# RWKV-7 chunk inverses in a diffusion backbone: the masked product copied into the inverse by four predicated copies, and other pauses around the products of inverses

## Chip, cores and metric

The kernel runs on one core of one Trainium2 chip. The metric is the device time of one execution in microseconds (us), shown as the median of three runs.

## What is computed

A backbone block with two layers over 256 context and 1024 latent tokens of width 1024, all in float32. Each layer has an input projection, three groups of heads (a gated linear attention, a windowed attention, and RWKV-7 time mixing in both directions), an output projection and a SwiGLU. The change lies in the RWKV group, whose recurrence the reference writes token by token:

```
def rwkv7_scan(r, w, k, v, kk, a, state0):
    def step(S, inp):
        rt, wt, kt, vt, kkt, at = inp
        sa = jnp.einsum('bhvk,bhk->bhv', S, kkt)
        S = (S * wt[:, :, None, :] - sa[..., None] * (kkt * at)[:, :, None, :]
             + vt[..., None] * kt[:, :, None, :])
        return S, jnp.einsum('bhvk,bhk->bhv', S, rt)
    S_final, o = lax.scan(step, state0, xs)
```

There are 4 heads of 64, two directions, and the state is a 64x64 matrix of each head.

## The kernel before

**The chunks.** The kernel works on chunks of 64 tokens, 20 in each layer. Within a chunk the recurrence becomes a triangular system of 64x64, one for each of the 4 heads and 2 directions; its inverse is needed. `u` counts four pairs (2 directions by 2 pairs of heads), and the two heads of a pair, or the halves of a block, lie on different partitions. Everything below is in the function `rwkv_mixer`.

**`prep` (L1183 on)** is a generator that makes the inverses. Iteration `i` begins the "young" chunk `i` and ends the "old" chunk `i - 1`, so that the two share instructions. In the order of the code:

1. `gram` multiplies the young chunk's four vectors on TensorE (`ps_g`) and VectorE multiplies the result by a triangular mask into `LQ` (128 partitions x 4 x 128). `X`, the inverse to be, starts as an identity of 32x32 blocks, written by GpSimd (`eye32`).
2. The first level of the inverse is the masked part of `LQ` itself. ScalarE copies its four 32x32 diagonal blocks, one for each group of 32 partitions, into a tile `ld`; one predicated copy on VectorE writes `ld` into `X` where the mask `lev1` is set; a VectorE transpose of 32x32 blocks makes `XT` (L1199 to L1203).
3. The old chunk's second Gram product goes to `MP` in the same way. GpSimd scales `Ke`.
4. `yield 3400`: see below.
5. Two steps, each of them: `py = LQ * XT` (`ps_y`, 32x32 products, 16 or 32 instructions), a ScalarE copy to `y`, `yield 1000`, `pz = y * X` (`ps_w`), a predicated copy of `pz` into `X` with the mask `lev2`, a transpose to `XT`, `yield 1200`. Step 0 and step 1 serve the young and the old chunk at once, which are at different levels.
6. For the old chunk a last product joins the 32x32 blocks to 64x64: 8 instructions of `ps_y` (called ps_y6 in the code), 4 transposes `ps_kt`, 8 of `ps_w`; the result is `XF`.

**`scan` (L1272 on)** follows with the state: `ps_r` from `MP` and from the state `SBD`, copies to `Rbd`, `ps_r` again with `XF`, copies to `VU` and `Ubd`, `ps_s`, and the state's update. Chunk `i` of the scan needs the inverse `i` and the scan of `i - 1`. `finish` normalizes a tile of finished tokens, with many small VectorE operations (`bn_stats`, a square root by integer arithmetic `rw_rs`, `fy`).

**`in_rest`** is the dense work beside it: the other 13 columns of the input projection, with 24 products of 128x128 by 512 (or 256) for each column and group of tokens (`ps_in`), each column with its own weight split (`w_hl`), drains, rotary positions (`rope`, L657 to L664) and the gates of the linear attention (`gl_`). The last column is held back until the scan has ended (`HOLD = 1`).

**What sets the order.** Class `Weave` runs these generators against each other and so writes TensorE's program by hand. `Tensor` keeps a count of modelled TensorE time `TE.t`; a generator that yields a number of ns is not resumed before that much modelled time has gone by, and whoever is ready by rank goes first: scan 0, prep 1, finish 3, dense work 9. So a pause in `prep` is filled with dense products, as long as there are any. The instructions of ScalarE, VectorE, GpSimd and the queues are put in order by the framework's own scheduler; those that `prep` and `scan` issue (`FIRST`) have a raised priority. All engines then run in their order and wait on semaphores.

Of the kernel before, what the change touches and what calls it, by code (L numbers as in the profile page):

```python
# [10 lines left out]
F32 = mybir.dt.float32  # L11
# [27 lines left out]
P = 128  # L39
# [106 lines left out]
def block_kernel(ctx: ExitStack, tc: tile.TileContext, a):  # L146
    nc = tc.nc
    V, S, G, SY = nc.vector, nc.scalar, nc.gpsimd, nc.sync
# [973 lines left out]
    def rwkv_mixer(l, t_first, pool, fpool, pp, spawn):  # L1122
# [7 lines left out]
        lev1 = pool.tile([P, 128], U8, name="lev1")  # L1130
# [19 lines left out]
        f2 = lambda ap: ap.rearrange("p u n -> p (u n)")  # L1150
# [5 lines left out]
        def gram(AK, w_, dst):  # L1156
            V = FIRST[0]
            ps = new([P, 4, P], "ps_g")
            for u in range(4):
                for hs in H:  # L1160
                    TE.matmul(ps[hs, u, :], AK[hs, u, w_, :], AK[hs, u, 0:2, :].rearrange("p s n -> p (s n)"))
            V.tensor_tensor(dst.rearrange("p (d q) n -> p d q n", d=2), ps.rearrange("p (d q) n -> p d q n", d=2),
                            mgr.unsqueeze(2).to_broadcast([P, 2, 2, P]), ALU.mult)
# [3 lines left out]
        def load(i):  # L1167
            b, cc = batch[i], (i, SIGC[i])

            AK = pool.tile([P, 4, 4, 64], F32, name="AK", bufs=4)  # L1170
            for d in range(2):
                SY.dma_start(AK[:, 2 * d:2 * d + 2], d_ab[:, 2 * d:2 * d + 2, cc[d]])
            Dt = pool.tile([P, 4], F32, name="Dt", bufs=4)
            for d in range(2):
                G.tensor_copy(Dt[:, 2 * d:2 * d + 2].unsqueeze(2), Dall[l][:, 2 * d:2 * d + 2, cc[d]:cc[d] + 1])
            b.update(cc=cc, AK=AK, Dt=Dt)
# [6 lines left out]
        def prep():  # L1183

            V, S, G = FIRST
            load(0)
            for i in range(NC + 1):
                yield after(("s", i - 3))
                p = i % 2
                young, old = batch[i] if i < NC else None, batch[i - 1] if i else None  # L1190
                hv = slice(0, 2) if i < NC and i else slice(p, p + 1) if old is None else slice(1 - p, 2 - p)
                if young is not None:
                    if i + 1 < NC:
                        load(i + 1)
                    X, XT = X2[:, p], XT2[:, p]
                    G.tensor_copy(X, eye32.unsqueeze(1).to_broadcast([P, 4, 32]))
                    young["LQ"] = LQ = pool.tile([P, 4, P], F32, name="LQ", bufs=3)
                    gram(young["AK"], 3, LQ)
                    ld = pool.tile([P, 4, 32], F32, name="ld")  # L1199
                    for r in range(0, 128, 32):  # L1200
                        S.copy(ld[r:r + 32], LQ[r:r + 32, :, r % 64:r % 64 + 32])
                    V.copy_predicated(f2(X), lev1, f2(ld))
                    V.transpose(f2(XT), f2(X))  # L1203
                if old is not None:
                    cc, Dt, AK = (old[n] for n in ("cc", "Dt", "AK"))
                    old["VU"] = VU = pool.tile([P, 512], F32, name="VU", bufs=3)
                    old["vb"] = vb = Vbd[p]
                    for d in range(2):
                        c = cc[d]
                        src = d_v[c % 2 * 64:c % 2 * 64 + 64, c // 2, :]  # L1210
                        SY.dma_start(VU[0:64, d * 256:(d + 1) * 256], src)
                        s4 = src.rearrange("s (q h n) -> s q h n", q=2, h=2)
                        for hp in range(2):
                            SY.dma_start(vb[H[hp], 2 * d:2 * d + 2, H[hp]], s4[:, :, hp, :])

                    Ke = pool.tile([P, 4, P], F32, name="Ke")
                    G.tensor_tensor(Ke, AK[:, :, 2:4, :].rearrange("p u w n -> p u (w n)"),
                                    Dt.unsqueeze(2).to_broadcast([P, 4, P]), ALU.mult)
                    old["MP"] = MP = pool.tile([P, 4, P], F32, name="MP", bufs=2)
                    gram(AK, 2, MP)  # L1220
                yield 3400 if young is not None else 0
                both = [(h, b["LQ"]) for h, b in ((p, young), (1 - p, old)) if b is not None]
                for step in range(2):
                    py = new([P, 2, 4, 32], "ps_y")
                    for h, LQ in both:
                        for u, rs, cs in blocks:
                            TE.matmul(py[rs, h, u, :], LQ[rs, u, cs], XT2[rs, h, u, :])
                    y = pool.tile([P, 2, 4, 32], F32, name="y", bufs=2)
                    S.copy(y[:, hv], py[:, hv])
                    yield 1000  # L1230
                    pz = new([P, 2, 4, 32], "ps_w")
                    for h, LQ in both:
                        for u, rs, cs in blocks:
                            TE.matmul(pz[rs, h, u, :], y[rs, h, u, :], X2[rs, h, u, :])
                    V.copy_predicated(f3(X2[:, hv]), lev2[:, step, p, hv].rearrange("p h n -> p (h n)"), f3(pz[:, hv]))
                    V.transpose(f3(XT2[:, hv]), f3(X2[:, hv]))
                    yield 1200
                if old is None:
                    continue

                X, XT, LQ, xf = X2[:, 1 - p], XT2[:, 1 - p], old["LQ"], XF[p]
                for r in (0, 32, 64, 96):
                    (S.copy if r < 64 else G.tensor_copy)(xf[r:r + 32, :, r % 64:r % 64 + 32], X[r:r + 32])
                ab = [(h, v, d) for v in range(2) for d in range(2) for h in (0, 64)]
                py = new([P, 2, 32], "ps_y6")
                for h, v, d in ab:
                    ra, rb = (h, h + 32) if d == 0 else (h + 32, h)
                    TE.matmul(py[rb:rb + 32, v, :], LQ[ra:ra + 32, 2 * d + v, rb % 64:rb % 64 + 32],
                              XT[ra:ra + 32, 2 * d + v, :])
                y = pool.tile([P, 2, 32], F32, name="y6")  # L1250
                S.copy(y, py)
                pt = new([P, 4, P], "ps_kt")
                for u in range(4):
                    TE.transpose(pt[:, u, :], Ke[:, u, :], eye)
                old["KT"] = KT = pool.tile([P, 4, P], F32, name="KT", bufs=2)
                S.copy(KT, pt)
                yield 300
                pz = new([P, 2, 32], "ps_w6")
                for h, v, d in ab:
                    ra, rb = (h, h + 32) if d == 0 else (h + 32, h)  # L1260
                    TE.matmul(pz[ra:ra + 32, v, :], y[rb:rb + 32, v, :], X[rb:rb + 32, 2 * d + v, :])
                for h in (0, 64):
                    for d in range(2):
                        ra, rb = (h, h + 32) if d == 0 else (h + 32, h)
                        (V.tensor_copy if d == 0 else S.copy)(
                            xf[ra:ra + 32, 2 * d:2 * d + 2, rb % 64:rb % 64 + 32], pz[ra:ra + 32])
                old["X"] = xf
                at["b", i - 1] = TE.t + 900
# [83 lines left out]
        for rank, gen in ((0, scan()), (1, prep()), (3, finish_all())):  # L1352
            spawn(gen, rank, LEAD[l])
# [582 lines left out]
```

## Time and profile before

| what | us |
|---|---|
| three runs | 3725.49, 3730.49, 3733.39 (median 3730.49) |
| the profiled execution | 3721.78 |
| its span in the trace | 3719.8 |
| TensorE busy, over the span | 3548.3 (95%) |
| VectorE busy | 2347.6 (63%) |
| ScalarE busy | 1518.4 (41%) |
| GpSimd busy | 693.1 (19%) |

The chunks of layer 0 run from 256 us to about 709 us of the span, those of layer 1 from 2253 to about 2690; between them lie the windowed attention, the linear attention, the output projection, the SwiGLU and the next layer's input. In the profile PE is TensorE, DVE VectorE, ACT ScalarE, POOL GpSimd, SP the queue that issues DMAs. Most matmuls of the kernel are recorded by one helper, so their line is always L160 and they are told apart by their tiles; a float32 product is recorded as two instructions or more, so the counts of the trace are twice those of the program for small products.

### The profile page before, as it was taken

The page shows a single profiled execution, that of the slowest core. Times are in us where ns is not written, and L with a number is a line of the kernel's source. Part 1 is how long each engine was busy: PE and PEld are TensorE (multiplying, and loading weights), DVE is VectorE, ACT ScalarE, POOL GpSimd, SP SyncE. Part 2 cuts the span into 40 slices and gives each one's busy share as a digit, 9 for nine tenths or more (in the row PEclk, how much of TensorE's full clock was granted, in tenths as well). Part 3 has the DMA queues.
Part 4 walks back from the last instruction along what each step waited for, and adds up shares of the span by engine and source line. Part 5 has one row for each costly group of instructions (what it writes and reads, how often), then busy time and mean ns, then how long its engine had stood idle before and what let it go on. Part 6 is the DMA issues. An engine that isn't in the chain of part 4 may idle for free. (4 is left out here: it accounts for less than half of the span.)

```text
span 3719.8 us, 76157 instructions
## 1 busy us (share of the span) xinstructions
PE 3548.3 (95%) x30714; PEld 2800.8 (75%) x30714; DVE 2347.6 (63%) x4516; ACT 1518.4 (41%) x3094; POOL 693.1 (19%) x979
## 2 busy tenths in 40 slices
PE   7988899999999999999999998989899999999998
PEld 4766778656788888888788766777777778888787
DVE  4764555556557777746776783455665676666766
ACT  4434543346324333333442543553366143333213
POOL 3122332111333000000341232232211340000002
PEclk8999999999999999999999999999989999999999
DMA  5253343553331333325421234343321332221611
GB/s 184 105 171 102 110 141 95 138 146 91 98 107 60 109 115 110 112 76 195 133 90 59 83 141 141 114 141 105 95 80 47 122 104 87 82 88 57 204 63 63
DMA packets 310768, 405.78 MB, mean 109 GB/s; under 512 B 52880, under 2 KB 210192, under 8 KB 308368
## 3 DMA queue, kind: packets, MB, share of 16 engines
q1 hardware_dynamic: 310416, 400.92, 34.3%
q8 instruction: 242, 3.96, 0.4%
q14 instruction: 110, 0.90, 0.1%
HBM read 290.54 MB, written 105.03 MB: 106 GB/s over the span
## 5 line engine op out<-in xcount | busy, mean ns | idle before, releaser
L160 PE MATMUL ps_in<-h,w_hl 128*128 128x512 f32 (+1 forms) x2928 | 708.1, 382 | 9.3 <-ACT w_hl L412 2.7
L160 PEld LDWEIGHTS ps_in<-h,w_hl 128*128 128x128 f32 x2928 | 486.6, 192 | 135.7 <-issue 52.1
L160 PE MATMUL ps_gu<-f,hl 128*128 128x512 f32 (+1 forms) x2400 | 566.4, 388 | 7.5 <-DVE hl L413 4.2
L160 PE MATMUL ps_d<-g,w_hl 128*128 128x512 f32 (+1 forms) x2688 | 556.2, 368 | 9.1 <-DVE x L1700 6.7
L160 PEld LDWEIGHTS ps_d<-g,w_hl 128*128 128x128 f32 x2688 | 462.9, 189 | 102.8 <-DVE x L1700 11.3
L160 PEld LDWEIGHTS ps_gu<-f,hl 128*128 128x128 f32 x2400 | 441.2, 189 | 102.2 <-DVE hl L413 5.1
L1700 DVE SCALAR_TENSOR_TENSOR x<-ps_d,mods,x 128x512 f32<-128x512 f32 (+1 forms) x448 | 291.0, 684 | 131.3 <-PE ps_d L160 130.7
L160 PE MATMUL ps_gu<-T,hl 128*128 128x512 f32 x1440 | 346.9, 390 | 1.5 <-DVE u L1601 1.5
L160 PEld LDWEIGHTS ps_gu<-T,hl 128*128 128x128 f32 x1440 | 268.8, 188 | 57.6 <-ACT g L412 1.9
L277 POOL TENSOR_TENSOR ada<-ada 128x256 f32<-128x256 f32 x112 | 89.2, 830 | 690.1 <-DMA x<-d_gt 557.2
L365 POOL TENSOR_TENSOR nacc<-nacc,nsq 128x512 f32<-128x512 f32 (+1 forms) x52 | 60.8, 1169 | 759.6 <-ACT nsq L364 744.6
L412 ACT CAST hl<-S 128x512 fp32r<-128x512 f32 x160 | 98.4, 620 | 249.4 <-PE ps_gu L160 155.8
L412 ACT CAST w_hl<-w_raw 128x1024 fp32r<-128x1024 f32 (+1 forms) x100 | 100.9, 1013 | 235.9 <-PE ps_d L160 199.3
L412 ACT CAST hl<-raw 128x512 fp32r<-128x512 f32 x156 | 96.6, 622 | 219.2 <-PE ps_gu L160 196.2
L1044 DVE TENSOR_REDUCE mx<-ps_ss 128x1 f32<-128x640 f32 (+2 forms) x144 | 107.5, 747 | 115.0 <-PE ps_ss L160 114.6
L160 PE MATMUL ps_o<-m,w_hl 128*128 128x512 f32 (+1 forms) x720 | 169.7, 383 | 0.0
L413 DVE TENSOR_TENSOR hl<-S,hl 128x512 fp32r<-128x512 f32 x160 | 110.0, 689 | 64.9 <-ACT hl L412 64.4
L160 PEld LDWEIGHTS ps_o<-m,w_hl 128*128 128x128 f32 x720 | 124.6, 191 | 31.0 <-issue 7.7
L413 DVE TENSOR_TENSOR w_hl<-w_raw,w_hl 128x1024 fp32r<-128x1024 f32 (+1 forms) x100 | 120.3, 1207 | 40.8 <-ACT w_hl L412 40.5
L413 DVE TENSOR_TENSOR pT<-ps_st,pT 128x512 fp32r<-128x512 f32 (+1 forms) x168 | 109.0, 657 | 33.4 <-ACT pT L412 32.9
L160 PEld LDWEIGHTS ps_x<-f,hl 128*128 128x128 f32 x960 | 124.5, 191 | 6.6 <-issue 0.8
L160 PE MATMUL ps_x<-f,hl 128*128 128x256 f32 x960 | 127.1, 283 | 0.0
(354 smaller groups left out, 5937.9 us busy)
## 6 DMA issues: line engine op xcount, KB each, us to landing
w_raw<-in_w_in_dram SPq DMA_DIRECT2D x44, 512.0 KB, 3.7
raw<-in_w_gate_dram SPq DMA_DIRECT2D x44, 512.0 KB, 3.5
raw<-in_w_up_dram SPq DMA_DIRECT2D x44, 512.0 KB, 3.7
x<-d_gt SPq DMA_DIRECT2D x88, 256.0 KB, 3.2
AK<-d_ab SPq DMA_DIRECT2D x80, 256.0 KB, 3.8
w_raw<-in_w_down_dram SPq DMA_DIRECT2D x40, 512.0 KB, 3.6
d_gt<-u SPq DMA_DIRECT2D x68, 256.0 KB, 2.2
d_ab<-W SPq DMA_DIRECT2D x16, 1024.0 KB, 3.9
```

The lines of the kernel that those rows point to most:

```text
L160: return nc.tensor.matmul(out, lhsT, rhs, **kw)
L277: G.tensor_tensor(acc[:, s], acc[:, s], ps_[n % 2], ALU.add)
L365: (G if 0 < o < 5 else V).tensor_tensor(self.acc[g0], self.acc[g0], sq[:, :n], ALU.add)
L412: S.copy(dst[:, 0], src)
L413: V.tensor_tensor(dst[:, 1], src, dst[:, 0].bitcast(F32), ALU.subtract)
L1044: V.tensor_reduce(m_, psf[:, :nk * P], AX.X, ALU.max)
L1700: V.scalar_tensor_tensor(x[:, o, g0:g0 + n], ps[:, :n], mods[:, l, s, 40 + o:41 + o], x[:, o, g0:g0 + n], ALU.mult, ALU.add)
```

## The change

The four ScalarE copies, the tile `ld` and the one predicated copy are replaced by four predicated copies that read `LQ` directly, one for each group of 32 partitions. The pause behind the Gram products becomes 3000 instead of 3400, the pause behind each product of inverses 1900 instead of 1200.

```diff
--- before.py
+++ after.py
@@ -1196,10 +1196,9 @@
                     G.tensor_copy(X, eye32.unsqueeze(1).to_broadcast([P, 4, 32]))
                     young["LQ"] = LQ = pool.tile([P, 4, P], F32, name="LQ", bufs=3)
                     gram(young["AK"], 3, LQ)
-                    ld = pool.tile([P, 4, 32], F32, name="ld")
                     for r in range(0, 128, 32):
-                        S.copy(ld[r:r + 32], LQ[r:r + 32, :, r % 64:r % 64 + 32])
-                    V.copy_predicated(f2(X), lev1, f2(ld))
+                        V.copy_predicated(X[r:r + 32], lev1[r:r + 32].rearrange("p (u n) -> p u n", n=32),
+                                          LQ[r:r + 32, :, r % 64:r % 64 + 32])
                     V.transpose(f2(XT), f2(X))
                 if old is not None:
                     cc, Dt, AK = (old[n] for n in ("cc", "Dt", "AK"))
@@ -1218,7 +1217,7 @@
                                     Dt.unsqueeze(2).to_broadcast([P, 4, P]), ALU.mult)
                     old["MP"] = MP = pool.tile([P, 4, P], F32, name="MP", bufs=2)
                     gram(AK, 2, MP)
-                yield 3400 if young is not None else 0
+                yield 3000 if young is not None else 0
                 both = [(h, b["LQ"]) for h, b in ((p, young), (1 - p, old)) if b is not None]
                 for step in range(2):
                     py = new([P, 2, 4, 32], "ps_y")
@@ -1234,7 +1233,7 @@
                             TE.matmul(pz[rs, h, u, :], y[rs, h, u, :], X2[rs, h, u, :])
                     V.copy_predicated(f3(X2[:, hv]), lev2[:, step, p, hv].rearrange("p h n -> p (h n)"), f3(pz[:, hv]))
                     V.transpose(f3(XT2[:, hv]), f3(X2[:, hv]))
-                    yield 1200
+                    yield 1900
                 if old is None:
                     continue
```

How it moves instructions, at three places. First TensorE in layer 0, in the middle of a chunk (`ps_s` and `ps_r<-Ubd` are the scan's, `ps_in` the dense products, `x6` or `x9` their count). Before:

```order
L160 MATMUL ps_s<-VU,KT 128x128 x4
L160 MATMUL ps_r<-Ubd,LQ 64x128 x4
L160 MATMUL ps_in<-h_334,w_hl 128x512
L160 MATMUL ps_y<-XT_1828,LQ 32x32 x32
L160 MATMUL ps_in<-h_334,w_hl 128x512 x5
L160 MATMUL ps_w<-X_1827,y 32x32 x32
L160 MATMUL ps_in<-h_334,w_hl 128x512 x2
L160 MATMUL ps_in<-h_408,w_hl 128x512 x4
L160 MATMUL ps_y_6119<-XT_1828,LQ 32x32 x8
L164 MATMUL ps_kt<-cst,Ke 128x128 x4
L160 MATMUL ps_in<-h_408,w_hl 128x512 x2
L160 MATMUL ps_w_6139<-X_1827,y_6128 32x32 x8
```

And in the change, at the corresponding place:

```order
L160 MATMUL ps_s<-VU,KT 128x128 x4
L160 MATMUL ps_r<-Ubd,LQ 64x128 x4
L160 MATMUL ps_in<-h_334,w_hl 128x512 x2
L160 MATMUL ps_y<-XT_1828,LQ 32x32 x32
L160 MATMUL ps_in<-h_334,w_hl 128x512 x5
L160 MATMUL ps_w<-X_1827,y 32x32 x32
L160 MATMUL ps_in<-h_334,w_hl 128x512 x9
L160 MATMUL ps_y_6196<-XT_1828,LQ 32x32 x8
L164 MATMUL ps_kt<-cst,Ke 128x128 x4
L160 MATMUL ps_in<-h_334,w_hl 128x512 x2
L160 MATMUL ps_w_6216<-X_1827,y_6205 32x32 x8
```

Between the step's `ps_w` and the 8 instructions of `ps_y` that follow it there are nine dense products, where there were six.

Second, TensorE in layer 1 near the end of the scan, from the scan's `ps_s` of the third chunk from the end on. Before:

```order
L160 MATMUL ps_s<-VU,KT 128x128 x4
L160 MATMUL ps_r<-Ubd,LQ 64x128 x4
L160 MATMUL ps_in<-h_20940,w_hl 128x512 x2
L160 MATMUL ps_y<-XT_22396,LQ 32x32 x32
L160 MATMUL ps_in<-h_20940,w_hl 128x512 x5
L160 MATMUL ps_w<-X_22395,y 32x32 x32
L160 MATMUL ps_in<-h_20940,w_hl 128x512 x2
L160 MATMUL ps_in<-h_20802,w_hl 128x512 x4
L160 MATMUL ps_y_28537<-XT_22396,LQ 32x32 x8
L164 MATMUL ps_kt<-cst,Ke 128x128 x4
L160 MATMUL ps_in<-h_20802,w_hl 128x512 x2
L160 MATMUL ps_w_28557<-X_22395,y_28546 32x32 x8
```

And in the change:

```order
L160 MATMUL ps_s<-VU,KT 128x128 x4
L160 MATMUL ps_r<-Ubd,LQ 64x128 x4
L160 MATMUL ps_y<-XT_22356,LQ 32x32 x32
L160 MATMUL ps_w<-X_22355,y 32x32 x32
L160 MATMUL ps_y_28486<-XT_22356,LQ 32x32 x8
L164 MATMUL ps_kt<-cst,Ke 128x128 x4
L160 MATMUL ps_w_28504<-X_22355,y_28495 32x32 x8
L160 MATMUL ps_g<-AK 64x128 x16
L160 MATMUL ps_r<-Vbd_22345,MP 128x128 x4
L160 MATMUL ps_r<-SBD,AK 128x128 x4
L164 MATMUL ps_f<-cst,fy 128x128 x2
L160 MATMUL ps_r<-Rbd,XF_22347 64x128 x4
```

The dense products have ended in the change; the next ones stand behind the scan's last instruction. Before, 33 stand between this place and the scan's end, 15 of them in the rows shown.

Third, VectorE in layer 0, from the Gram's mask to the copy for the scan. Before:

```order
L177 TENSOR_TENSOR LQ<-ps_g,c_mgr 128x512
L177 TENSOR_TENSOR MP<-ps_g,c_mgr 128x512
L177 COPY_PREDICATED X_1827<-lev_1792,ld 128x128
L177 STREAM_TRANSPOSE XT_1828<-X_1827 128x128
L413 TENSOR_TENSOR w_hl<-w_raw,w_hl 128x1024
L177 COPY Rbd<-ps_r 64x4x64
```

And in the change:

```order
L177 TENSOR_TENSOR LQ<-ps_g,c_mgr 128x512
L177 COPY_PREDICATED X_1827<-lev_1792,LQ 32x128 x4
L177 TENSOR_TENSOR MP<-ps_g,c_mgr 128x512
L177 STREAM_TRANSPOSE XT_1828<-X_1827 128x128
L177 COPY Rbd<-ps_r 64x4x64
```

The four predicated copies follow `LQ` at once, and the mask of `MP` has moved behind them, ahead of the transpose.

## Rows read from the trace of the kernel before

**Rows 1.** The page: its span, and the first engine of its table of busy time.
```profile
span 3719.8 us, 76157 instructions
...
PE 3548.3 (95%) x30714; PEld 2800.8 (75%) x30714; DVE 2347.6 (63%) x4516; ACT 1518.4 (41%) x3094; POOL 693.1 (19%) x979
```

**Rows 2.** Busy time by engine in the chunk stretches: stretch, length, us (instructions), granted clock, DMA.
```profile
256.00:709.00 453.00, 418.11 (x8177) 336.51 (x8178) 232.33 (x665) 201.97 (x500) 115.92 (x196) 0.98 0.40 116
2253.00:2690.00 437.00, 402.87 (x8028) 322.38 (x8028) 218.28 (x603) 194.55 (x480) 109.93 (x190) 0.97 0.39 112
```

**Rows 3.** TensorE's waits, 255 to 800, then 2250 to 2700: total us, times, longest.
```profile
PE ps_y L160 <- DVE XT L177: 13.9, 9, 3.2
...
PE ps_y L160 <- DVE XT L177: 12.1, 8, 3.5
```

**Rows 4.** Timeline of TensorE, first and last such wait: start, us, what, [idle before].
```profile
270.77 0.45 PE L160 MATMUL ps_y<-XT,LQ 32*32 32x32 f32 x32 [3.18 <-DVE XT L177]
...
2581.74 0.33 PE L160 MATMUL ps_y<-XT,LQ 32*32 32x32 f32 x16 [1.20 <-DVE rw_rs_y L443]
```

**Rows 5.** Timeline of all engines in one chunk of layer 0.
```profile
424.26 0.69 DVE L177 TENSOR_TENSOR LQ<-ps_g,c_mgr 128x512 f32<-128x512 f32 x1 [0.58 <-PE ps_g L160]
424.98 1.22 ACT L177 COPY ld<-LQ 32x128 f32<-32x128 f32 x4 [1.28 <-DVE LQ L177]
...
425.13 0.69 DVE L177 TENSOR_TENSOR MP<-ps_g,c_mgr 128x512 f32<-128x512 f32 x1 [0.18 <-PE ps_g L160]
...
426.30 0.31 DVE L177 COPY_PREDICATED X<-lev,ld 128x128 f32<-128x128 uint8 x1 [0.48 <-ACT ld L177]
...
426.65 0.31 DVE L177 STREAM_TRANSPOSE XT<-X 128x128 f32<-128x128 f32 x1
...
428.84 0.75 PE L160 MATMUL ps_y<-XT,LQ 32*32 32x32 f32 x64
...
430.98 0.75 PE L160 MATMUL ps_w<-X,y 32*32 32x32 f32 x64
...
431.77 0.45 DVE L177 COPY_PREDICATED X<-lev,ps_w 128x256 f32<-128x256 uint8 x1 [0.37 <-PE ps_w L160]
432.26 0.45 DVE L177 STREAM_TRANSPOSE XT<-X 128x256 f32<-128x256 f32 x1
```

**Rows 6.** Timeline of all engines, a wait behind a product in layer 0.
```profile
440.81 1.22 DVE L660 TENSOR_TENSOR t<-t,rope 128x512 f32<-128x512 f32 x1
...
443.00 0.44 DVE L177 STREAM_TRANSPOSE XT<-X 128x256 f32<-128x256 f32 x1
...
443.59 0.33 PE L160 MATMUL ps_y<-XT,LQ 32*32 32x32 f32 x16 [2.69 <-DVE XT L177]
```

**Rows 7.** Busy time behind two such waits; the granted clock stands third from the end.
```profile
271.00:274.40 3.40, 3.40 (x67) 2.45 (x54) 0.17 (x1) 0.64 (x2) 0.00 (x0) 0.54 0.67 176
2441.90:2445.30 3.40, 3.18 (x44) 2.43 (x46) 1.20 (x4) 1.59 (x5) 1.53 (x3) 0.53 0.95 317
```

**Rows 8.** VectorE's groups by shape, 250 to 720: count, busy us, mean ns, idle before.
```profile
L177 DVE COPY XF<-ps_w 32x64 f32<-32x64 f32 x40 | 8.7, 216 | 27.0 <-PE ps_w L160 26.7
...
L177 DVE COPY_PREDICATED X<-lev,ld 128x128 f32<-128x128 uint8 x20 | 6.1, 305 | 10.3 <-ACT ld L177 9.0 <-issue 1.3
...
L443 DVE SCALAR_TENSOR_TENSOR rw_rs_y<-rw_rs_t,rw_rs_y 128x4 f32<-128x4 f32 x30 | 4.1, 166 | 0.0
```

**Rows 9.** Busy time at both scans' ends, and timeline rows of layer 1's.
```profile
2655.00:2677.50 22.50, 16.44 (x361) 13.78 (x347) 13.57 (x56) 9.00 (x26) 6.72 (x11) 1.00 0.19 53
664.00:687.00 23.00, 22.35 (x297) 18.89 (x295) 9.58 (x24) 8.12 (x21) 3.52 (x6) 1.00 0.40 106
...
2657.35 0.33 PE L160 MATMUL ps_y<-XT,LQ 32*32 32x32 f32 x16 [1.84 <-DVE rw_rs_t L442]
...
2677.49 11.19 PE L160 MATMUL ps_in<-h,w_hl 128*128 128x512 f32 x48
```

## Prediction

> **What bounds the kernel now.** I read the page's head first. TensorE is busy for 95% of the span [rows 1], so an edit pays only where TensorE stands idle, or where it runs at the lower of its two clocks. The change lives in the two stretches in which RWKV's chunks run beside the dense input products; the busy-time table of both shows TensorE busy for 418.1 of 453 us in layer 0 and for 402.9 of 437 in layer 1 [rows 2]. So 34.9 and 34.1 us of idle time are there, and no edit of these pauses can win more than that and what the clock adds.
>
> Next, who ended that idle time: the table of waits. The largest entry in both stretches is `ps_y` waiting for the transpose into `XT`: 13.9 and 12.1 us in 17 waits [rows 3]. In layer 1 two more are put down to the group-norm's square root, which stood beside the transpose on VectorE: 1.20 us [rows 4] and 1.84 [rows 9]. That makes 29.0 us in 19 waits. I went through the timeline and sorted them by the pause in front of them. Two stand behind the Gram product (the pause of 3400), together 1.1 us. Three stand in the last two chunks of a layer, together 3.3. The other 14, from the first of 3.18 us to the last of 1.20 [rows 4], stand behind a product of inverses (the pause of 1200); none is under 0.88, and their sum is 24.7 us.
>
> Then one chunk in detail, to see why [rows 5]. The Gram's masked sum `LQ` ends at 424.95; four ScalarE copies take 1.22; the predicated copy starts at 426.30 and the transpose ends at 426.96; TensorE comes for it at 428.84, 1.9 us later. So the pause of 3400 is too long by nearly 2 us in an ordinary chunk. Behind the product the predicated copy and the transpose take 0.45 each, and `XT` is there 0.97 us after the product's last row (431.73 to 432.71). The pause of 1200 covers that by about half a microsecond, and fails when something large stands before them on VectorE. Such a case: the rotary multiplication of 1.22 us, then the transpose's end at 443.44, then `ps_y` at 443.59 after 2.69 us of idling [rows 6].
>
> **The change, part by part.**
>
> *Four predicated copies instead of four ScalarE copies and one.* VectorE loses 40 copies of 0.305 us and gets 160. No row shows a predicated copy of 32 partitions. The nearest from below is VectorE's 32-partition copy of 64 elements, 0.216; from above the 128-partition predicated copy of the same 128 elements, 0.305 [rows 8]. I take 0.305, since a row's length and not its number of partitions is what it shares with it. Four take 1.22 us, exactly what the ScalarE copies took [rows 5], and the hand-over from ScalarE to VectorE falls away. But in the order of the change `MP`'s masked sum (0.69 us) now stands between the four copies and the transpose, in nearly every chunk; in the order of before it stood in front of the one copy, beside ScalarE's work. So `XT` comes as early as before, within some 0.1 us. The 120 x 0.305 = 36.6 us more of VectorE lie in stretches where it works half the time (232.3 of 453 us [rows 2]), and the 40 x 1.22 = 49 us of ScalarE that go stood in front of none of these waits: both are costed at nothing. The cover is the 1.9 us above.
>
> The sequence has a rule against it. By the Trainium skill ("VectorE: DVE Perf Modes", section on two Vector instructions with no wait between them), an instruction whose input starts at another quadrant of partitions than the last one's is held until the earlier ones have ended; the four copies start at four quadrants, so none overlaps. That agrees with pricing them end to end; were they to overlap down to 0.216, `XT` would be 0.36 us earlier and the next term 0 instead of 0.5.
>
> *Pause of 3400 to 3000.* TensorE comes 0.4 us earlier; of 1.9 us some 1.5 remain. Only places that are late already lose: two, 0.4 each at most. Term: +0.5 us (0 to 1.5).
>
> *Pause of 1200 to 1900.* The order of the change has nine dense products where there were six, in front of the last transposed product of a chunk. A dense product takes 11.19/48 = 0.233 us [rows 9], so three are 0.7. Each of the 14 waits shrinks by this and none is shorter: 14 x 0.68 = 9.5 us. The bound is the 24.7 they hold.
>
> *Where the large VectorE operations stand.* In layer 0 the order of before has a rotary multiplication or its sum around the copy behind a product in five places; the change's has one, the others stand behind the Gram product now, where 1.5 us are to spare. Against that, the split of a weight stands between copy and transpose in seven places instead of three. I take -3 us (0 to -8).
>
> *The clock.* Five of the waits for `XT` were followed by a stretch of some 3.4 us at a granted clock of about half, 1.2 instead of 2.4 GHz; the first and the last stand in [rows 7]. A stretch like that costs half of its length, 1.7. With 0.7 us less idling I count one as saved: -1.7 us (0 to -8.5).
>
> *The end of the scan, where the cover goes.* What is now spent in the middle is missing at the end. In layer 1 the order of before has 33 dense products between the place shown and the scan's end, that of the change has none; in layer 0 the last chunk loses all it had, 22 products with 512 columns and 24 with 256. The held-back column must wait for the scan and cannot fill it. The trace has both cases: layer 0's last chunk with dense work stood idle for 0.65 of 23 us, layer 1's without for 6.1 of 22.5, of which 1.84 belong to the chunk ahead [rows 9]. So an uncovered last chunk costs 4.2. Layer 0: 4.2 - 0.65 = +3.6. Layer 1: one and a half further chunks, at least one at 4.2, at most 1.5 at 5.0 (its steps are twice as wide, and copy and transpose take 0.45 instead of 0.31 each): 4.2 to 7.5, I take +6.
>
> **Sum**: -9.5 - 3 - 1.7 + 0.5 + 3.6 + 6 = -4.1 us. The profiled execution took 3721.78 us, its span 3719.8, so it would be 3717.7. It was 8.7 below the median of the three runs, 3730.49; against the median the forecast is 3726.4, say 3726.
>
> **Rivals.**
>
> *The end dominates (slower).* Without dense work TensorE waits for the whole VectorE queue, and there the group-norm of finished tiles is queued too: some 26 small operations of 0.166 us each [rows 8], 4.3 us in a row, which the order of the change has in front of a predicated copy in two of layer 1's last four chunks. That they hurt is shown by the 1.84 us in [rows 9]. If they come on top in both, the end costs 3.6 + 7.5 + 8.6 = 19.7, against 9.5: +10.2, about 3741. It decides when the idle time of the last chunks grows by more than the waits shrink. Against it: VectorE runs much of this while TensorE does the scan's own products. Chance 0.2.
>
> *The waits vanish (faster).* The 0.7 us and the better order together remove the 14 waits to 17.5 us, and the clock stays up all five times: -17.5 - 8.5 + 7.8 = -18, 3712. For it: the rotary work has gone from these places. Against: seven weight splits have come. Chance 0.25.
>
> *Nothing is bought.* The in-order queues of ScalarE and VectorE meet at other places; the waits for `y` (ScalarE's table loads) and `VU` grow by what those for `XT` shrink. 3730, chance 0.1. A variant belongs to the new copies: they need the identity that GpSimd writes into `X`, and ScalarE's 1.22 us used to hide a late one.
>
> *The forecast*, a gain of 0 to 9 us: 0.45.
>
> **How the numbers follow.** About 0.2% (7.5 us) is what a measurement of this kernel can tell from no change; faster means under 3723. A quarter of the forecast's cases and nearly all of the fast rival lie there: 0.11 + 0.24 = 0.35. Slower, over 3738: some three quarters of the first rival, 0.16, and a little of the others: 0.18. The rest, 0.47, is the same. The range reaches from the fast rival's 3712 to 3742: a mere 4 us won of the waits, against an end of 3.6 + 7.5 + 4.3.
>
> **What would show it.** In the profile of the change: `ps_y` behind `XT` falls from 29 us to some 12 to 18 over both stretches; 160 predicated copies of about 0.3 us and no `ld`; `XT` ready some 2 us behind the Gram product as before; idle time of 4 us or more in layer 0's last chunk, where 0.65 was, and over 10 in layer 1's last two and a half. It is wrong if the waits for `XT` stay at 25 us or more, if the end costs under 5 or over 15 us, or if a new wait (`y`, `VU`, `X` from GpSimd) grows by over 5.

## The result, and the profile after

The changed kernel takes 3758.89 us (median of 4 runs, 3753.51 to 3762.50) against 3731.20 for the kernel before on the same chip: a ratio of 1.0069, 95% interval 1.0052 to 1.0086. It is slower by 27.7 us where 4.1 us less was forecast, and above the range. The head of the page after, to set beside [rows 1]:

```profile
span 3751.3 us, 76093 instructions
...
PE 3558.9 (95%) x30714; PEld 2808.8 (75%) x30714; DVE 2378.4 (63%) x4636; ACT 1472.6 (39%) x2934; POOL 688.4 (18%) x979
```

VectorE has 120 instructions more and ScalarE 160 fewer, as the diff says. TensorE runs the same 30714 instructions in 10.6 us more of busy time: some of them ran slower. The rest of the 31.5 us of span is idle time.

**Where it went.** I cut each of the two stages at the last product of every chunk's scan, and grouped the 20 chunks: the first (the columns that run before it included), 2 to 9 (rotary positions and gates beside them), 10 to 17, the last three, and what is left behind the scan until the windowed attention begins. The table of busy time by stretch, kernel before, chunks 2 to 9, 10 to 17 and 18 to 20 of layer 0, then of layer 1 (start:end, length, PE busy, ...; PEclk is third from the end):

```profile
305.50:480.00 174.50, 155.00 (x3198) 121.80 (x3196) 86.89 (x222) 95.71 (x223) 50.24 (x89) 0.98 0.40 117
480.00:636.70 156.70, 146.73 (x3191) 119.91 (x3189) 89.88 (x246) 66.26 (x171) 46.48 (x77) 1.00 0.40 117
636.70:687.00 50.30, 49.65 (x902) 40.66 (x900) 25.70 (x95) 18.52 (x51) 12.08 (x21) 1.00 0.30 79
...
2300.00:2479.40 179.40, 160.24 (x3120) 126.16 (x3118) 84.70 (x175) 96.38 (x221) 49.54 (x89) 0.95 0.38 114
2479.40:2633.90 154.50, 149.17 (x3249) 120.64 (x3248) 82.81 (x239) 61.74 (x164) 43.29 (x75) 1.00 0.38 110
2633.90:2677.30 43.40, 37.34 (x830) 30.27 (x828) 24.42 (x92) 16.15 (x46) 12.92 (x21) 1.00 0.21 64
```

The same stretches of the changed kernel:

```profile
306.30:496.50 190.20, 164.32 (x3246) 130.01 (x3244) 102.27 (x255) 92.86 (x202) 53.21 (x90) 0.96 0.42 124
496.50:655.80 159.30, 153.23 (x3220) 125.23 (x3218) 86.20 (x261) 51.26 (x132) 40.65 (x75) 0.99 0.34 101
655.80:708.20 52.40, 45.76 (x850) 36.92 (x848) 27.00 (x97) 15.78 (x44) 11.85 (x21) 0.90 0.23 66
...
2317.40:2508.00 190.60, 165.45 (x3205) 127.86 (x3202) 94.95 (x202) 89.77 (x191) 53.67 (x87) 0.95 0.41 122
2508.00:2663.00 155.00, 151.31 (x3190) 122.09 (x3188) 86.26 (x259) 50.57 (x131) 41.28 (x74) 0.98 0.31 92
2663.00:2709.90 46.90, 34.11 (x797) 29.32 (x794) 23.76 (x93) 12.81 (x39) 11.82 (x21) 0.85 0.27 73
```

A stretch that holds more dense products may be longer, so lengths alone mislead. I took 11.19/48 = 0.233 us [rows 9] off each stretch for every dense product of 512 columns in it (one of 256 counts half). What is left is the price of the chunks themselves. Both layers together, before → after:

| chunks | dense products | length without them, us | TensorE idle, us | us at half clock |
|---|---|---|---|---|
| 1 | 183 → 198 | 54.0 → 50.5 | 7.6 → 6.0 | 16.3 → 12.3 |
| 2 to 9 | 412 → 466 | 257.9 → 272.2 | 38.7 → 51.0 | 23.9 → 31.7 |
| 10 to 17 | 432 → 455 | 210.5 → 208.3 | 15.3 → 9.8 | 0 → 9.3 |
| 18 to 20 | 113 → 52 | 67.4 → 87.2 | 6.7 → 19.4 | 0 → 23.9 |
| behind the scan | 139 → 107 | 3.2 → 2.7 | 1.3 → 0.9 | 0 → 0.1 |
| sum | 1279 → 1278 | 593.0 → 620.8 | 69.6 → 87.1 | 40.2 → 77.3 |

The two stages hold 27.8 of the 31.5 us by which the profiled span grew: 17.5 us of idle time, and some 10 us that go with 37 us more at half clock. The amount of dense work is fixed (1279 products). The longer pause moved some 90 of them forward, and the last three chunks were left with 52 instead of 113: the end is bare there, without the products that cover its waits.

These are two single executions, and the one of the kernel before was a quick one (3721.78 us, median 3731.20). The experiments below add three profiles with the old pause of 1200 everywhere (`copies_alone`, `copies_and_3000`, `before_cover2`) and three with 1900 everywhere (`copies_and_1900`, `pauses_alone`, `sv_3000`). Without their dense products chunks 2 to 9 take 257 to 262 us in the four with 1200 and 268 to 276 in the four with 1900, chunks 10 to 17 take 211 to 219 and 204 to 208, the last three 66 to 69 and 82 to 87; the time at half clock is 40 to 61 us and 77 to 92. So the two losses stand clear of the scatter, and the gain in chunks 10 to 17 is nearer 9 us (the difference of the means) than the 2.2 of this pair.

The table of waits of the changed kernel, layer 0 and below it layer 1 (waited for: total us, times, longest), to set beside [rows 3]:

```profile
PE ps_y L160 <- DVE XT L177: 11.8, 10, 2.3
PE ps_s L160 <- DVE VU L177: 8.4, 7, 2.0
PE ps_w L160 <- ACT y L177: 8.4, 11, 2.3
PE ps_tv L164 <- ACT in L630: 7.8, 1, 7.8
...
PE ps_y L160 <- DVE XT L177: 14.4, 15, 2.0
PE ps_tv L164 <- ACT in L630: 8.3, 2, 7.7
...
PE ps_y L160 <- DVE va L1328: 2.9, 1, 2.9
```

The waits for `XT` are 29.1 us (11.8 + 14.4 + 2.9) where they were 29.0, and a new one of 7.8 us stands in each layer: token transposes (`ps_tv`).

### The profile page after: what moved, and what is told of

It reads as the page before. It is cut to its first block, busy times and chain, and to the rows that moved or that the text cites. A ratio compares the mean times of both kernels' runs of the same rounds, so it can differ in the third digit from the quotient of the medians.

```text
span 3751.3 us, 76093 instructions
## 1 busy us (share of the span) xinstructions
PE 3558.9 (95%) x30714; PEld 2808.8 (75%) x30714; DVE 2378.4 (63%) x4636; ACT 1472.6 (39%) x2934; POOL 688.4 (18%) x979
## 5 line engine op out<-in xcount | busy, mean ns | idle before, releaser
L1044 DVE TENSOR_REDUCE mx<-ps_ss 128x1 f32<-128x640 f32 (+2 forms) x144 | 107.3, 747 | 110.6 <-PE ps_ss L160 110.0
```

The source lines that it names most:

```text
L1044: V.tensor_reduce(m_, psf[:, :nk * P], AX.X, ALU.max)
```

## The experiments

Each was timed against the kernel before on the same chip; the ratio is to that kernel. "1900" is the pause behind a product of inverses, "3000" the one behind the Gram products. The stretch figures come from one profiled execution of each. The expectations reckon with about 3731 us for the kernel before (3734 in the last one). Its median was 3734.19 beside the first four runs, 3738.75 beside the other lengths and the cover, and 3733.60 beside the runs on where the pause pays and on the new wait: so differences and ratios are to be compared with the expectations, not times.

### The change taken apart

Copies alone, pauses as before:

```diff
-                    ld = pool.tile([P, 4, 32], F32, name="ld")
-                        S.copy(ld[r:r + 32], LQ[r:r + 32, :, r % 64:r % 64 + 32])
-                    V.copy_predicated(f2(X), lev1, f2(ld))
+                        V.copy_predicated(X[r:r + 32], lev1[r:r + 32].rearrange("p (u n) -> p u n", n=32),
+                                          LQ[r:r + 32, :, r % 64:r % 64 + 32])
```

> Only the four predicated copies; the pauses stay 3400 and 1200, so TensorE's order is word for word that of before. Theory of the pauses (the order of TensorE, with its bare end and the shorter wait behind the Gram product, makes the loss): the same as before, 3725 to 3738 us. Theory of the copies (37 us more of VectorE, and MP's mask ahead of the transpose, make it): 10 to 25 us above before, 3741 to 3756. Theory of collisions (in-order queues meet at other places after any edit): anything within 12 us of before, with the token transpose's wait (ps_tv) the term that differs.

3738.16 us, ratio 1.0011 (0.9996 to 1.0026): not to be told from no change.

Copies with 3000 (`yield 3400` → `yield 3000`), and with 1900 instead (`yield 1200` → `yield 1900`):

> Copies, pause 3000 behind the Gram products, 1200 behind the products of inverses. The end of the scan keeps its dense products in both layers. If the bare end and its lower clock make most of the loss: 3728 to 3740 us. If the late XT behind the Gram product (11 us of waits in the change against 1) and the long wait of the token transposes make it: 3745 to 3758.

> Copies, pause 3400 behind the Gram products, 1900 behind the products of inverses. The waits behind the Gram product should go (from 11 us to under 4), while the end of the scan is still more bare than in the change (layer 1 loses its last 46 dense products). If the bare end makes the loss: 3750 to 3768 us. If the shorter pause of 3000 makes it: 3728 to 3745.

3739.39 us, ratio 1.0007 (0.9994 to 1.0021), and 3758.24 us, ratio 1.0051 (1.0036 to 1.0066). Both pauses without the copies:

> Only the pauses, 3000 and 1900, with the copies of before: TensorE's order is word for word that of the change. Theory of the pauses: as slow as the change, 3750 to 3765 us. Theory of the copies: 3725 to 3742, with XT some 1.9 us behind the Gram product again and few waits there. Theory of collisions: between 3735 and 3760, and the waits of the token transposes smaller than the change's 7.8 us.

3759.57 us, ratio 1.0061 (1.0042 to 1.0081). So the 1900 makes the loss, with the copies or without, and with 3000 or 3400; the other two edits cost nothing that these runs can tell. The new wait of the token transposes is no general cause: in `copies_and_1900` it is 1.3 us for ScalarE's `in`, and the loss is there. One expectation failed: in `copies_and_1900` the waits behind the Gram product should have fallen under 4 us, and they are 12.1.

### Other lengths of the pause

The changed kernel with 1550 and with 800 behind a product:

```diff
-                    yield 1900
+                    yield 1550
```

> The changed kernel with the pause behind a product at 1550 and not 1900, halfway to the 1200 of before (the other pause stays 3000, the copies stay). By the order of TensorE's queue the last five chunks of layer 0 hold 28, 29, 30, 27 and 18 dense products of 512 columns, those of layer 1 31, 28, 5, 0 and 0. Theory of the bare end: most of layer 0's 7.9 us comes back and little of layer 1's 11.0, while the waits behind the products grow by half of the 15.5 us that the change took from them: about the changed kernel's time or a little below, 3750 to 3758 us. Rival, the middle grows with the length of the pause: half of the whole loss, 3744 to 3750. Rival, a meeting of queues that only 1900 makes (the 7.8 us wait of the token transposes): near the kernel before, 3735 to 3742.

3755.57 us, ratio 1.0043 (1.0027 to 1.0058). The time does not decide: 16.8 us above the kernel before on this chip lie where the rival had it (half of the loss, 13 to 19 us above 3731), just under the bare end's 19 to 27, and the interval reaches both. The trace speaks for the bare end: without their dense products the last three chunks take 82.0 us (67.4 before), of which layer 1's take 48.3 (35.7). With half the lengthening layer 1's last three chunks already hold 5 dense products instead of 33.

> The changed kernel with the pause behind a product at 800, shorter than the 1200 of before (the other pause 3000, the copies stay). By the order of TensorE's queue every chunk of both scans keeps its dense products (last five chunks 22, 24, 23, 19, 28 in layer 0 and 24, 24, 28, 20, 30 in layer 1). Theory of the bare end: layer 1's end, which costs the kernel before 6.1 us of idle time, is covered, while the waits behind the products grow by 400/700 of the 15.5 us that 700 took from them, 8.9 us: 3731 + 9 - 6 = 3732 to 3740 us. Rival, the pause works by the waits behind the products alone, as the change means it: 3740 to 3747. Rival, a longer pause costs everywhere in the middle and a shorter one gives that back at the same rate (+8.7 us net of the middle for 700): 3722 to 3728.

3771.75 us, ratio 1.0080 (1.0063 to 1.0097): no theory foresaw that. The end is indeed covered (64.9 us against 67.4). But chunks 10 to 17 take 240.6 us without their dense products, 30 more than before. Busy time of these chunks, layer 0 and layer 1:

```profile
487.30:649.10 161.80, 147.84 (x3157) 119.78 (x3155) 94.56 (x270) 55.90 (x138) 44.59 (x77) 0.96 0.37 107
2500.80:2669.10 168.30, 153.12 (x3155) 122.51 (x3153) 95.95 (x273) 58.13 (x141) 48.48 (x79) 0.93 0.36 108
```

Idle time is 29.2 us (15.3 before), and 37.6 us run at half clock (none before). I had scaled the waits by the pause in a straight line. In fact 1200 leaves an ordinary chunk 0.55 us between the end of the transpose into `XT` and TensorE's use of it; 400 less leaves 0.15, and that is also what stands there wherever TensorE waits. At 800 TensorE starts with no more than this to spare in 35 of 40 chunks; at 1200 in 14.

### Giving the end its cover back

The changed kernel, with the held-back column let loose three chunks earlier, then the kernel before with one chunk earlier:

```diff
-        return after(("s", NC - 1))
+        return after(("s", NC - 4))
```

> The changed kernel, with the next block's dense products let loose three chunks earlier: the gate at the end of the mixer is chunk NC-4 of the scan and no longer chunk NC-1. By the order of TensorE's queue the last five chunks of layer 0 then hold 29, 32, 28, 27.5 and 35.5 products of 512 columns (29, 32, 28, 23 and 0 in the changed kernel), those of layer 1 27, 28, 26, 22 and 0 (27, 28, 0, 0, 0). Theory of the bare end: the changed kernel's loss is mostly the uncovered end of the two scans, 7.9 us in layer 0 and 11.0 us in layer 1 as read from its trace, and the part at half clock goes with it; all of layer 0's and most of layer 1's come back: 3738 to 3745 us, idle time of TensorE in layer 0's last three chunks under 2 us (6.6 in the changed kernel), in layer 1's last three under 8 (12.8). Rival, the middle of the stage: the longer pause costs by the waits it makes behind the Gram products, on the token transposes and by lower clock, all of it before the last three chunks, and the end is a small part: 3752 us or more, with the idle time at the end gone all the same. A third way: the products taken from behind the scan leave the loads of the windowed attention bare (up to the 10.9 us that 48 products of 0.227 us covered there in layer 1): 3748 to 3755 with a gap at the first scores of the window.

3771.89 us, ratio 1.0084 (1.0066 to 1.0102): not faster than the change, whose interval it overlaps. The end comes back just as the theory has it: the last three chunks take 67.6 us without their dense products (87.2), in layer 0 without a gap. But the products came from behind the scan, and there the normalization of the last tokens stood bare. Busy time of layer 0's last three chunks and of the stretch behind, then the waits behind the scan, layer 0 and layer 1:

```profile
655.00:706.20 51.20, 51.16 (x902) 41.36 (x900) 27.63 (x99) 17.56 (x48) 11.90 (x21) 1.00 0.21 61
706.20:719.90 13.70, 6.33 (x26) 4.27 (x24) 11.37 (x64) 3.95 (x10) 0.33 (x2) 0.76 1.11 239
```

```profile
PE ps_f L164 <- DVE fy L1332: 7.3, 2, 6.6
...
PE ps_f L164 <- DVE fy L1332: 8.3, 2, 7.6
```

That stretch takes 19.0 us without its dense products, 2.7 in the changed kernel: of 19.6 us won, 16.3 are paid at the next place. It is the third way of the expectation, but not by the loads that I had named; TensorE waits for VectorE's `fy`. The time, 33 us above the kernel before, is as long as the rival had it; the trace shows that chunks 2 to 9 and 10 to 17 take what they took in the change (270 and 209 us without their dense products, 272 and 208 there), so both hold: the middle keeps its loss, and that of the end has moved.

> The kernel before, with the same gate one chunk earlier (NC-2): 31 dense products of 512 columns come into layer 1's last chunk, where there were none, and 17 are left behind the scan (48 before); layer 0 keeps its order. Theory of the bare end: layer 1's end costs the kernel before 6.1 us of idle time in its last three chunks, and most of it goes: 3725 to 3729 us against 3731. Rival, the middle: the end has no price worth speaking of: 3730 to 3733. Third way, the loads of the windowed attention lose their cover: 3733 to 3738.

3737.54 us, ratio 0.9996 (0.9980 to 1.0013): too close to no change to decide between the three. In the trace it is the same exchange, smaller: the last three chunks 65.9 us (67.4), behind the scan 10.2 (3.2), with 6.3 us of waiting for `fy` in layer 1.

### Where the pause pays and where it costs

Copies, 3400, and 1900 in one part of the stage only:

```diff
-                    yield 1200
+                    yield 1900 if 9 <= i <= 16 else 1200
```

> Copies and the first pause of before (3400), and the longer pause behind a product, 1900, only where the index of the prepared chunk is 9 to 16; 1200 before and after. By the order of TensorE's queue layer 0 keeps its end (last five chunks 29, 29, 25, 23, 32 dense products of 512 columns) and layer 1 loses one chunk of it (29, 30, 9, 0, 0; 27, 30, 27, 6, 0 with 1200 everywhere). Theory of the ledger: these chunks (10 to 17 by my count) are the only ones in which 1900 buys anything; with the copies alone they took 219 us beyond 0.227 us for each dense product over both layers, with the change 211, so -6 to -8 there, and +5 to +6 for the one more bare chunk at layer 1's end: 3732 to 3740 us, a ratio to before of 1.000 to 1.002. Rival, the longer pause costs wherever it stands (by lower clock and by the work that it brings in front): 1.003 to 1.006.

3741.61 us, ratio 1.0021 (1.0007 to 1.0036), on the border between the two, a little slower than the kernel before. The trace tells the layers apart. In layer 0, whose end keeps its products, chunks 10 to 17 take 101.3 us without theirs (107.3 before), and the stage is 6.2 us shorter than before; in layer 1 they take 101.4 (103.2), and the end, with 9 products instead of 33, takes 43.8 (35.7).

> The complement: copies, 3400, and 1900 behind a product only where the index of the prepared chunk is 8 or less, 1200 from there on. By the order of TensorE's queue the last five chunks of layer 0 hold 26, 26, 32, 25 and 18 dense products, those of layer 1 29, 28, 5, 0 and 0. Theory of the ledger: 5 to 10 us lost in chunks 2 to 9, where the rotary and gate chains run, 1 to 2 at layer 0's end and about 11 at layer 1's, which goes bare although no pause near it is longer: 3752 to 3762 us, ratio 1.005 to 1.007. Rival, the long pauses near the end make the end's loss themselves: 3740 to 3748, ratio 1.002 to 1.003.

(`1900 if i <= 8 else 1200`.) 3753.26 us, ratio 1.0057 (1.0042 to 1.0072). Layer 1's chunks 10 to 17 and its last three, all of which have the old pause:

```profile
2504.10:2659.00 154.90, 149.27 (x3250) 120.78 (x3248) 87.99 (x262) 50.98 (x131) 42.48 (x74) 1.00 0.33 94
2659.00:2705.90 46.90, 35.29 (x801) 29.69 (x800) 24.10 (x93) 13.72 (x40) 12.14 (x21) 0.85 0.22 63
```

The last three stand idle for 11.6 us and run at a mean clock of 0.85, though the pause there is 1200. The products that are missing here were spent some ten chunks earlier. That decides between the theories: the end is lost by the sum of the pauses, not by those near it. In chunks 2 to 9 the pause bought nothing either: 267.1 us without the dense products (257.9 before, 262.4 with the copies alone).

### The new wait

The changed kernel with a longer pause ahead of the token transposes of the `sv` column:

```diff
             elif nm == "sv":
-                yield 1300
+                yield 3000
```

> The changed kernel with the pause between the eviction of the sv column and its token transposes at 3000 and not 1300, so that other products stand ahead of the transposes that waited 7.8 us for ScalarE in each layer. Theory, the wait is a head-of-queue wait and can be filled: both 7.8 us waits go or fall under 3 us, and 5 to 11 us come back: 3748 to 3754, ratio 1.004 to 1.005. Rival, ScalarE's and VectorE's chain (the gate's tables, the rotary products) holds the next product of inverses as long: the wait turns up under another name and the time stays, 3756 to 3762. What this does not touch, in either case, is the end of the two scans, some 19 us.

3763.50 us, ratio 1.0084 (1.0067 to 1.0100): the rival holds. Waits, layer 0 and below it layer 1:

```profile
PE ps_w L160 <- ACT y L177: 12.1, 10, 3.1
...
PE ps_tv L164 <- ACT in L630: 5.3, 1, 5.3
...
PE ps_w L160 <- ACT y L177: 9.4, 9, 2.1
...
PE ps_tv L164 <- ACT in L630: 6.0, 1, 6.0
```

The two long waits lose 4.2 us (15.5 to 11.3), and those for `y`, which ScalarE writes too, grow by 5.9 (15.6 to 21.5). So what is late is the chain of ScalarE and VectorE, as far as one profiled execution tells; it is not that the transposes come early.

### A version that beats both

The kernel before with 1900 where it pays alone:

```diff
-                    yield 1200
+                    yield 1900 if l == 0 and 9 <= i <= 16 else 1200
```

> The kernel before with one line changed: behind a product of inverses 1900 and not 1200 where the index of the prepared chunk is 9 to 16, in layer 0 alone; no other part of the change. By the order of TensorE's queue both scans then end as in the kernel before (layer 0's last five chunks 29, 29, 25, 23 and 32 dense products, with 64 left behind the scan where 92 stood; layer 1 27, 30, 27, 6, 0). Theory of the ledger: chunks 10 to 17 of layer 0 take 103 us beyond their dense products as in late_1900, 109 in the kernel before and 112 with the copies alone, and nothing is paid for it at an end: 6 to 9 us faster, 3725 to 3729 us against 3734, ratio 0.9975 to 0.9985. Rival, what the pause saves there comes back at half clock or behind the scan: ratio 0.9995 to 1.0015.

3728.34 us (12 runs) against 3734.74, ratio 0.9979 (0.9969 to 0.9990): faster, as forecast. Layer 0's chunks 10 to 17, its last three, and the stretch behind the scan:

```profile
482.80:640.00 157.20, 152.49 (x3223) 124.43 (x3222) 90.39 (x251) 67.36 (x175) 46.21 (x79) 1.00 0.41 119
640.00:689.90 49.90, 49.65 (x897) 40.17 (x895) 25.82 (x93) 18.21 (x50) 11.91 (x21) 1.00 0.25 74
689.90:705.80 15.90, 15.65 (x83) 13.02 (x80) 12.43 (x65) 6.10 (x15) 1.53 (x2) 1.00 1.04 216
```

The idle time of chunks 10 to 17 falls from 10.0 to 4.7 us at full clock. The products for it come from behind the scan, where 92 stood and 64 are enough.

## Why the prediction was wrong, by its own steps

Two steps failed. The waits that were to go in the middle (-9.5, -3 and -1.7 us) were booked as time won, and they came back at other places; and the end of the scan, priced at 9.6 us, cost 19.8.

**Copies: the price right, the delay mis-sized.** Four predicated copies in a row take 1.23 us, where 1.22 was forecast. In the chunk below `XT` is ready 2.28 us behind the end of `LQ`, 2.01 in [rows 5]: 0.27 us later, where within 0.1 was forecast. `copies_alone` shows that this costs no time that can be told. One chunk of VectorE's timeline in the changed kernel, which answers to [rows 5]:

```profile
340.00 0.69 DVE L177 TENSOR_TENSOR LQ<-ps_g,c_mgr 128x512 f32<-128x512 f32 x1 [0.43 <-PE ps_g L160]
340.80 1.23 DVE L177 COPY_PREDICATED X<-lev,LQ 32x128 f32<-32x128 uint8 x4
342.06 0.69 DVE L177 TENSOR_TENSOR MP<-ps_g,c_mgr 128x512 f32<-128x512 f32 x1
342.67 0.30 DVE L177 STREAM_TRANSPOSE XT<-X 128x128 f32<-128x128 f32 x1
```

Four times 0.31 us: the copies, each at another group of 32 partitions, do not overlap. That is what the rule named in the prediction says (the Trainium skill, "VectorE: DVE Perf Modes", section "Two Vector instructions with no wait between them").

**Pause of 3000, +0.5 us (0 to 1.5): right in time, as far as can be told, and wrong in the wait.** `copies_and_3000` cannot be told from `copies_alone` (3739.39 and 3738.16 us), though the waits behind the Gram product are 10.4 us in its trace, 5.6 with the copies alone and 1.1 before.

**Pause of 1900, -9.5 us: the waits went, the time did not.** In an ordinary chunk the time to spare behind a product rises from 0.55 to 1.2 us, by 0.65 where 0.68 was forecast. The waits that the step counted, 24.7 us behind the products outside a layer's end, fall to about 8, by more than the 9.5 (and than the 12.5 with the next step's 3). What failed is to book that as time won: TensorE's idle time falls by 5.5 us in chunks 10 to 17, but rises by 12.3 in chunks 2 to 9. There the last product's waits fall by 5.2 us, while 7.6 come up behind the Gram product, where none stood, and those ahead of `ps_tv` grow by 10.7 (5.7 to 16.4, whatever they wait for). The next two points are these.

**"Where the large VectorE operations stand", -3 us: this step failed.** It said that they stand behind the Gram product now, where 1.5 us are to spare. The waits there rose from 1.1 us to 11.1, in 12 places. One of them, VectorE's queue and then TensorE:

```profile
319.33 0.69 DVE L177 TENSOR_TENSOR MP<-ps_g,c_mgr 128x512 f32<-128x512 f32 x1
319.94 0.68 DVE L712 TENSOR_TENSOR_SCAN gl_u<-cst,gl_z 128x256 f32<-128x256 f32 x1
320.54 0.67 DVE L660 TENSOR_TENSOR t<-t,rope 128x512 f32<-128x512 f32 x1
...
321.12 0.30 DVE L177 STREAM_TRANSPOSE XT<-X 128x128 f32<-128x128 f32 x1
...
321.57 0.74 PE L160 MATMUL ps_y<-XT,LQ 32*32 32x32 f32 x64 [1.81 <-DVE XT L177]
```

A scan of the gate and the rotary product stand between `MP` and the transpose: together 1.35 us. I had counted one operation at a time against the 1.5. Neither of the other two edits is needed for it: these waits are 10.9 us in `pauses_alone`, with ScalarE's copies, and 12.1 in `copies_and_1900`, with 3400. Nor are they the loss by themselves: `copies_and_3000` has 10.4 us of them at the time of the kernel before.

**A wait that I did not look for.** Of my rivals' "queues meet at other places" the largest is `ps_tv` waiting for ScalarE's `in`, 4.7 us before and 16.1 after, all of it in chunks 2 to 9:

```profile
349.50 1.22 DVE L660 TENSOR_TENSOR t<-t,rope 128x512 f32<-128x512 f32 x1
350.82 0.92 DVE L661 TENSOR_TENSOR in<-in,t 128x512 f32<-128x512 f32 x1
...
351.77 0.62 ACT L663 CAST qk_hl<-in 128x512 fp32r<-128x512 f32 x1 [2.40 <-DVE in L661]
352.29 0.37 ACT L630 COPY in<-ps_in 128x256 f32<-128x256 f32 x1
...
352.71 0.69 PE L164 MATMUL ps_tv<-cst,in 128*128 128x128 f32 x2 [7.80 <-ACT in L630]
```

The eviction that the transposes need stands on ScalarE behind a cast that waits for VectorE's rotary sum, which waits behind the gate's chain. `sv_3000` shows that to move the transposes only moves the wait. The waits for `VU`, which the prediction did name as a sign, rose from 6.2 to 12.8 us.

**"The end of the scan", +9.6: the mechanism right, mis-sized by half.** It measured 19.8 us. Of that 12.7 are idle time, where I had 9.6. The rest is the clock, which I had looked for behind the waits in the middle only. Layer 0's last chunk, and 6.8 us of it:

```profile
690.70:708.20 17.50, 11.64 (x144) 9.78 (x142) 5.18 (x15) 3.97 (x12) 3.25 (x6) 0.71 0.29 82
...
694.60:701.40 6.80, 5.99 (x54) 5.16 (x54) 1.38 (x5) 1.80 (x6) 0.58 (x2) 0.51 0.00 0
```

The chunk stands idle for 5.9 of 17.5 us (0.65 of 23 in [rows 9]) and runs at a mean clock of 0.71. The step priced an uncovered chunk by layer 1's end in the kernel before, which happened to keep the full clock: in `copies_alone`, with TensorE's order of the kernel before, layer 1's last three chunks ran at half clock for 3.4 us.

**The clock, -1.7: wrong in sign.** The time at half clock rose from 40.2 to 77.3 us, in these stages.

**Sum and rivals.** In the place of the -4.1 stand the rows of the table above: +14.3 in chunks 2 to 9, -2.2 in 10 to 17, +19.8 at the end, -4.0 in the first chunk and behind the scan. "The end dominates" had the end at 19.7, and 19.8 was measured, but that is luck: 8.6 of the 19.7 were group-norm operations in front of the inverse, to which the table of waits puts down 2.9 (`va`), and the clock filled the rest. It also kept the gain in the middle and so came to 3741. "Nothing is bought" came nearest in the middle, which in fact lost. I treated them as alternatives, with 0.3 for both; they came together. The bounds I set myself were crossed as they should be: the waits for `XT` at 25 us or more, the end over 15, a new wait over 5.

What stays open: why 1900 lowers no idle time in chunks 2 to 9. The eight profiled orders with a pause other than 1200 there take 267 to 276 us without their dense products, the six with 1200 take 257 to 262. Which meeting of queues costs that was not taken apart. The waits behind the Gram product stand in all eight (6 to 13 us in these chunks), but 6.7 us stand in `copies_and_3000` too, which loses nothing; the long wait of `ps_tv` stands in four of the eight. In `early_1900` the idle time there is hardly longer than before (40.5 us, 38.7), and the time at half clock is (44.4, 23.9).

## What to carry to other kernels

Work that fills pauses is a fixed stock: before a pause is lengthened, count what it takes (here 0.7 us, two or three products, at each chunk's last step) and find the place that is left without, at the far end of the stage, whichever pause spent it. Price that place with its clock as well as its waits. And lengthen the pause only where both an ordinary wait is left and stock is over: in layer 0's quiet chunks that won 0.2%, where 1900 in all chunks, with the other edits or without, lost 0.5 to 0.7%.

## What the runs showed that was not expected

The clock fell in chunks in which no wait is long. Here is TensorE's timeline in the changed kernel, one row of the middle at full clock and then the end of layer 0:

```profile
343.86 1.06 PE L160 MATMUL ps_r<-SBD,AK 128*128 128x128 f32 x8
...
693.15 0.45 PE L160 MATMUL ps_y<-XT,LQ 32*32 32x32 f32 x32 [2.25 <-DVE XT L177]
693.99 0.45 PE L160 MATMUL ps_w<-X,y 32*32 32x32 f32 x32 [0.39 <-ACT y L177]
695.31 0.43 PE L160 MATMUL ps_y<-XT,LQ 32*32 32x32 f32 x16 [0.87 <-DVE XT L177]
...
698.95 1.92 PE L160 MATMUL ps_r<-SBD,AK 128*128 128x128 f32 x8
```

No wait of this chunk is over 2.25 us, and from 694.6 to 701.4 the granted clock is 0.51, the lower of the two levels (1.2 GHz); the same eight products of `ps_r` take 1.92 us there and 1.06 in the middle. In the kernel before, layer 1's last chunks with waits of up to 1.84 us kept the clock at 1.00 [rows 9]; in `copies_alone` the same order of products lost it for 3.4 us. So the waits in the middle are not the only place where the clock has to be priced; what decides whether it falls these runs do not show.
